# A hybrid decoder on one core: y groups copied out by ScalarE, exponentials held from the third query split, x's first tile issued first

## The chip, the core and the metric

The kernel runs on one core of one Trainium2 chip. The core has a matrix engine (TensorE, PE in the profile; its weight loads are PEld), a vector engine (VectorE, DVE), an activation engine (ScalarE, ACT), a general engine (GpSimd, POOL) and a queue engine that here only issues DMAs (SyncE, SP). Every engine works through its own instructions in a fixed order. The metric is the device time of one execution in microseconds; the figure of a kernel is the median of its runs.

## The reference

The input is x with 256 positions of 2048 features in float32. Two layers follow.

```
layer 0:  x += recurrent_block(rms_norm(x));  x += swiglu_ffn(rms_norm(x))
k, v   =  split(rms_norm(x) @ w_kv), k normalised per head        # 4 heads of 64
layer 1:  x += attention(rms_norm(x), k, v);  x += swiglu_ffn(rms_norm(x))
```

The recurrent block splits `rms_norm(x) @ w_in` in a y branch and an x branch of 2048 each. The x branch passes a causal convolution of width 4, two block diagonal gates with sigmoids, and a linear recurrence over the positions; its result times gelu(y) goes through `w_out`. Attention has 32 query heads of 64, each query normalised per head, a causal window of 128, and a sink per head in the softmax. The feed-forward width is 5632.

## The kernel before, in words

**Layout.** Features lie on the 128 partitions, the 256 positions along the free dimension, so a vector of 2048 features is 16 tiles of 128x256. A product in float32 is made of three products of a shorter format: each operand is split in a high part and the low remainder, and high times high, high times low and low times high are summed in a bank of PSUM. For an activation the split is `split_act` (L419): ScalarE copies the high part, VectorE subtracts. `gained` (L425) does the same with the norm's gain: it reads a tile of x and a column of the parameter tile `par`, ScalarE first, VectorE after it.

**The stream of weights.** All weights pass in 704 tiles of 128x1024 (512 KB), in one long list `jobs`. `stream` (L278) goes through it: `load` (L231) issues the DMA of the tile four ahead on SP's queue, `split` (L259) makes `hi` on ScalarE (L264) and `lo` on VectorE (L267) for the tile three ahead, and the job's own function issues 24 matmuls of 256 columns (L330, L328). Four buffers each hold `raw`, `hi` and `lo`. `warm` (L269) runs 15 matmuls on zeros before the first tile. In `load` for tile 0, ScalarE's queue issues two small DMAs: 16 columns of `par` (L238) and the first tile of x (L239).

**Groups.** `group` (L347) makes a group of 512 output features: 8 jobs (22 for the output of the feed-forward layer), at the end of which `done` gets four results in banks of PSUM; there are 8 banks. With a non-empty `sync`, the first two results of a group have two halves in one bank that must be added (`two`). `pull` (L401) takes a result out of its bank: with `two`, ScalarE copies one half and VectorE adds; without, VectorE multiplies by `rstd` straight from the bank if `r` is given, and ScalarE copies if not. Then the bank is free.

**The planner.** The work between matmuls is written as generators that are spawned in a list `bg`. `run_bg` (L203) steps the first one that is due, in the order of spawning, until the work issued in this tick, by estimated costs, passes `DVE_TICK` or `ACT_TICK`. A tick is half a job. A `yield` lets the budget be looked at, a `yield n` sets the generator aside for n ticks. If a job needs an operand that isn't issued yet, `need` (L216) steps all generators until it is. Program order is the priority from which the compiler's scheduler then fixes each engine's order, with its own estimate of when operands are ready.

**Recurrent block.** The order of jobs is `ORDER` (L54): x0 and x1 interleaved, x2, g0, x3, g1, y0, g2, g3, y1, g4, g5, y2, g6, g7, y3. x and y are groups, g are the gates, one job each (`gates`, L651), whose sigmoids free two banks per gate; `recur` (L684) then does the recurrence of two gates' tiles. `y_group` (L716) pulls its four results through `scaled` (L583), which multiplies by the norm's `rstd` once that is known, and its task computes gelu and the product with the recurrence (ScalarE's squares, VectorE's products, ScalarE's tanh, the final split). y0 and y2 have no `sync`, y1 and y3 have. The output projection (`lru_out`, `project`, L512) follows y3 at once and needs the split products in order.

**Attention.** `attn` (L868) has four groups of queries, each of four pairs of heads. At a group's end its task (L1012) squares the four results, splits them (`split_act`, L1022), sums the squares per head by small matmuls (L1031), copies the sums out with ScalarE into a tile `h` (L1034), transposes them on TensorE (L1039), makes the factors of the norm (`rsqrt`) and puts the four pairs in `todo`. The generator `pairs` (L946) visits TensorE every three ticks (`VISIT`): a visit issues the values of one pair (L881), the scores of a new one (L899) and the transposes of a third (L891). Between visits `softmax` (L910) takes the new pair: VectorE adds the mask and takes the row maximum (L918), ScalarE makes the exponentials (L929, L934), VectorE the reciprocal, GpSimd the sums and products (L940, L942). The flag `summing` stops the softmax before the maximum is negated (L925) while a query group's sums are on their way: it is set after the four splits (L1024) and cleared after the copy to `h` (L1035). The small float32 matmuls and transposes are issued through `pe_other` (L334), which keeps them in one chain. Most rows of the profile name a helper's line: L116 is every activation of ScalarE, L125, L129, L134 and L136 are VectorE's, L338 and L341 the small matmuls. The output projection of attention has its first two groups interleaved, so that a pair of value tiles is used for two jobs.

Of the kernel before, what the change touches and what calls it, by code (L numbers as in the profile page):

```python
# [15 lines left out]
ALU = mybir.AluOpType  # L16
# [3 lines left out]
T = 256  # L20
# [29 lines left out]
class Trunk:  # L50
# [180 lines left out]
    def load(self, i):  # L231
        dma = self.nc.sync.dma_start
        raw, src = self.raw[i % 4], self.jobs[i][0]
        if i == 0:

            other = self.nc.scalar.dma_start
            g = slice(C_N1A, C_N1A + 16)
            other(self.par[:, g], self.d["par"][:, g])  # L238
            other(self.x[0][:, 0:1, :], self.d["x"][:, 0:1, :])  # L239
            dma(raw[:, 0:512], src[:, 0:512])  # L240
            dma(self.x[0][:, 1:2, :], self.d["x"][:, 1:2, :])
            dma(raw[:, 512:1024], src[:, 512:1024])
        elif i == 1:
            dma(raw[:, 0:512], src[:, 0:512])
            dma(raw[:, 512:1024], src[:, 512:1024])
        else:
            dma(raw, src)

        if i == 0:
            self.xin = 2  # L250
        elif i % 2 and i < ND - 1:
            dma(self.x[(i + 1) // 4][:, (i + 1) % 4:(i + 1) % 4 + 2, :], self.d["x"][:, i + 1:i + 3, :])
            self.xin = i + 3
        elif i == 8:
            dma(self.par[:, C_N1A + 16:NPAR], self.d["par"][:, C_N1A + 16:NPAR])
        elif i == 10:
            dma(self.con, self.d["con"])
# [341 lines left out]
    def lru(self, gains, rn):  # L599
# [116 lines left out]
        def y_group(g):  # L716
            def done(ps):
                v = []
                for f in range(4):
                    o = self.half()  # L720
                    self.scaled(o, ps[f])
                    v.append(o)

                def task():
                    th = []
                    yield 1
                    for f in range(4):
                        s = self.slot(F32)
                        o = s[:, 0:T]
                        th.append((s, o))  # L730
                        self.a(o, v[f], AF.Square, scale=math.sqrt(0.044715 * GK))
                        yield
                    for f in range(4):
                        o = th[f][1]
                        self.stt(o, o, GK, v[f], ALU.add, ALU.mult)
                        self.a(o, o, AF.Tanh)
                        yield
                    for f in range(4):
                        s, o = th[f]
                        k = 4 * g + f  # L740
                        self.stt(o, o, 1.0, v[f], ALU.add, ALU.mult)
                        while not hs[k].ready:
                            yield 1
                        h = hs[k].ap[:, 0:T]
                        self.stt(o, o, 0.5, h, ALU.mult, ALU.mult)
                        yield
                        q = self.slot()
                        self.split_act(q, o)
                        self.free(s)
                        self.free(hs[k].ap)  # L750
                        self.free_half(v[f])
                        zs[k].ap = q
                        zs[k].ready = True
                        yield
                self.spawn(task())
            self.group(lambda c: w[g, c], ND, xs, done, g == 3, self.SYNC if g in (1, 3) else ())

# [110 lines left out]
    def attn(self, xs, r, gains, rn):  # L868
# [41 lines left out]
        def softmax(k, rr, ps, sc):  # L910
            f = k % 4
            sm = self.half()
            mx, nm, es, den = (sm[:, 4 * i:4 * i + 4] for i in range(4))
            for hh in range(2):
                for b, c0, c1 in blocks:
                    i = b * 2 + hh
                    self.dve += 69 + 1.042 * (c1 - c0)
                    nc.vector.tensor_tensor_reduce(  # L918
                        sc[hh][:, c0:c1], ps[hh][:, c0:c1], con[:, K_MASK + c0:K_MASK + c1],
                        rr[:, b * 8 + f * 2 + hh:b * 8 + f * 2 + hh + 1],  # L920
                        par[:, C_SINK + 4 * k + hh:C_SINK + 4 * k + hh + 1], ALU.add, ALU.max,
                        accum_out=mx[:, i:i + 1])
                self.free_mbank(ps[hh])
                yield
            while self.summing:  # L925
                yield 1
            self.ts(nm, mx, -1.0, None, ALU.mult)
            self.tt(es, par[:, C_SINK + 4 * k:C_SINK + 4 * k + 4], mx, ALU.subtract)
            self.a(es, es, AF.Exp)  # L929
            for hh in range(2):  # L930
                for b, c0, c1 in blocks:
                    i = b * 2 + hh
                    o = sc[hh][:, c0:c1]
                    self.a(o, o, AF.Exp, bias=nm[:, i:i + 1], accum_out=den[:, i:i + 1])  # L934
                yield
            self.tt(den, den, es, ALU.add)
            self.rcp(den, den)
            for hh in range(2):
                o = sc[hh][:, P:2 * P]
                nc.gpsimd.tensor_tensor(o, o, sc[hh][:, 2 * P:3 * P], ALU.add)  # L940
                o = sc[hh][:, 0:2 * P].rearrange("p (b q) -> p b q", b=2)
                nc.gpsimd.tensor_tensor(o, o, den[:, hh:4:2].unsqueeze(2).broadcast_to([P, 2, P]), ALU.mult)  # L942
                yield
            self.free_half(sm)
# [59 lines left out]
        for g in range(4):  # L1004
            def done(ps, g=g):
                v = []
                for p in ps:
                    s = self.slot(F32)
                    self.pull(p, s[:, 0:T])
                    v.append(s)  # L1010

                def task():  # L1012
                    while not self.rv[r].ready:
                        yield 1
                    rt = self.rstd[r][:, T:T + 2]
                    if g == 0:
                        self.stt(r2, rt, 1.0 / HD, rt, ALU.mult, ALU.mult)
                    qs = []
                    for f in range(4):
                        self.a(v[f][:, T:2 * T], v[f][:, 0:T], AF.Square)  # L1020
                        qs.append(self.slot())
                        self.split_act(qs[f], v[f][:, 0:T])  # L1022
                        yield
                    self.summing = True  # L1024
                    yield 1
                    while not self.room():
                        yield 1
                    p = self.mbank()

                    for f in range(4):  # L1030
                        self.pe_other(p[32 * f:32 * f + 32, 0:T], con[:, K_HS:K_HS + 32], v[f][:, T:2 * T],  # L1031
                                      start=True, stop=True)
                    h = self.half()
                    self.a(h, p[:, 0:T])  # L1034
                    self.summing = False  # L1035
                    yield
                    yield 1
                    for b in range(2):
                        self.pe_other(p[:, T + b * P:T + b * P + P], h[:, b * P:b * P + P], one, f=nc.tensor.transpose)  # L1039
                    self.free_half(h)  # L1040
                    yield 1
                    rr, m, t = (self.rrs[g][:, 16 * i:16 * i + 16] for i in range(3))
                    for b in range(2):
                        self.ts(m[:, 8 * b:8 * b + 8], p[:, T + b * P:T + b * P + P:16], r2[:, b:b + 1], EPS,
                                ALU.mult, ALU.add)
                    self.free_mbank(p)
                    for q in v:
                        self.free(q)
                    self.rsqrt(rr, m, t)
                    for b in range(2):  # L1050
                        self.ts(rr[:, 8 * b:8 * b + 8], rr[:, 8 * b:8 * b + 8], rt[:, b:b + 1],
                                1.0 / math.sqrt(HD), ALU.mult, ALU.mult)
                    yield
                    for f in range(4):
                        todo.append((4 * g + f, qs[f], rr))
                    if g == 0:
                        self.spawn(pairs())
                    yield
                self.spawn(task())
            self.group(lambda c, g=g: w[g, c], ND, xs, done, g == 3, self.SYNC, packed=True)  # L1060
# [100 lines left out]
```

## Time and profile before

| what | us |
|---|---|
| runs, median of three | 1982.1 (1980.66 to 1982.5) |
| the profiled execution, its own time | 1980.68 |
| its span, first to last instruction | 1978.9 |
| TensorE busy | 1971.8 |
| VectorE busy | 1256.3 |
| ScalarE busy | 1063.0 |
| GpSimd busy | 70.5 |

The granted clock of TensorE is 1.00 over the span. A row of a timeline gives start and length in us, engine, line and operation, the tiles written and read (`out<-in`, buffer numbers left out), shape and count, and in square brackets how long the engine sat idle just before and what ended that. Several instructions of one kind in a row are merged to one line. `b` is a bank of PSUM, `s` a general tile of 128x512, `h` a half-sized one. The recurrent block takes up to about 290 us, the first feed-forward layer lies behind it, attention with its projections between 1011 and 1270, and the second feed-forward layer takes the rest.

### The profile page before, as it was taken

The page shows a single profiled execution, that of the slowest core. Times are in us where ns is not written, and L with a number is a line of the kernel's source. Part 1 is how long each engine was busy: PE and PEld are TensorE (multiplying, and loading weights), DVE is VectorE, ACT ScalarE, POOL GpSimd, SP SyncE. Part 2 cuts the span into 40 slices and gives each one's busy share as a digit, 9 for nine tenths or more (in the row PEclk, how much of TensorE's full clock was granted, in tenths as well). Part 3 has the DMA queues.
Part 4 walks back from the last instruction along what each step waited for, and adds up shares of the span by engine and source line. Part 5 has one row for each costly group of instructions (what it writes and reads, how often), then busy time and mean ns, then how long its engine had stood idle before and what let it go on. Part 6 is the DMA issues. An engine that isn't in the chain of part 4 may idle for free.

```text
span 1978.9 us, 40162 instructions
## 1 busy us (share of the span) xinstructions
PE 1971.8 (100%) x16683; PEld 1930.5 (98%) x16683; DVE 1256.3 (63%) x1981; ACT 1063.0 (54%) x1606; POOL 70.5 (4%) x100
## 2 busy tenths in 40 slices
PE   9999999999999999999999999999999999999999
PEld 9999999999999999999999889999999999999999
DVE  8988876556556655545668776755655565554443
ACT  7798655444444444434556775544544454443342
POOL 0000000000000000000002461000000000000000
PEclk9999999999999999999999999999999999999999
DMA  8555655655556555555655335555565556666663
GB/s 289 185 180 189 212 190 190 197 194 192 192 194 195 196 192 193 192 195 196 195 183 180 130 128 168 190 196 192 192 193 196 196 190 196 193 195 204 208 205 126
DMA packets 106198, 377.10 MB, mean 191 GB/s; under 512 B 11936, under 2 KB 14368, under 8 KB 106016
## 3 DMA queue, kind: packets, MB, share of 16 engines
q1 hardware_dynamic: 105408, 373.88, 57.7%
q8 instruction: 130, 2.13, 0.4%
q10 hardware_dynamic: 608, 0.66, 0.1%
q14 instruction: 52, 0.43, 0.1%
HBM read 371.88 MB, written 2.10 MB: 189 GB/s over the span
## 4 chain that ended last, share of the span: by engine, by line
PE 97%; ACT 1%; DVE 1%; issue 0%; POOL 0%; DMA 0%; ACTq 0%; POOLq 0%
PE b L330 93%; PE b L341 1%; PE b L664 1%; ACT s L116 1%; PE b L338 1%; PE b L850 1%; DVE lo L267 0%; ACT hi L264 0%; DVE s L918 0%; PE b L859 0%; PE b L860 0%; PE b L861 0%; DMA x<-in_x 0%; DVE s L125 0%; DVE s L129 0%
## 5 line engine op out<-in xcount | busy, mean ns | idle before, releaser
L330 PE MATMUL b<-s,hi 128*128 128x256 f32 (+1 forms) x10329 | 1432.1, 284 | 1.1 <-DVE h L125 0.6
L330 PEld LDWEIGHTS b<-s,hi 128*128 128x128 f32 x10329 | 1316.8, 188 | 30.5 <-ACT s L116 1.2
L267 DVE TENSOR_TENSOR lo<-raw,hi 128x1024 fp32r<-128x1024 f32 (+1 forms) x707 | 861.5, 1220 | 655.0 <-ACT hi L264 652.6
L264 ACT ACTIVATE hi<-raw 128x1024 fp32r<-128x1024 f32 (+1 forms) x707 | 746.1, 1056 | 808.6 <-PE b L330 750.7
L330 PE MATMUL b<-s,lo 128*128 128x256 f32 x5504 | 827.9, 276 | 0.0
L330 PEld LDWEIGHTS b<-s,lo 128*128 128x128 f32 x5504 | 718.3, 188 | 0.6
L940 POOL TENSOR_TENSOR s<-s 128x128 f32<-128x128 f32 x32 | 14.8, 463 | 1100.4 <-ACT s L116 1097.6
L116 ACT ACTIVATE s<-h 128x256 fp32r<-128x256 f32 (+1 forms) x106 | 40.7, 411 | 23.5 <-DVE h L125 23.5
L116 ACT ACTIVATE t<-b 128x256 f32<-128x256 f32 x130 | 47.9, 375 | 4.1 <-PE b L330 1.7
L116 ACT ACTIVATE s<-x,par 128x256 fp32r<-128x256 f32 x80 | 38.9, 499 | 20.4 <-DVE x L125 13.7
L116 ACT ACTIVATE s<-s 128x256 f32<-128x256 f32 (+2 forms) x116 | 41.7, 412 | 10.9 <-DVE s L129 7.5
L116 ACT ACTIVATE h<-h 128x256 f32<-128x256 f32 (+1 forms) x104 | 38.9, 376 | 3.7 <-DVE h L125 1.5
L116 ACT ACT_TABLE_LOAD x30 | 38.5, 1283 | 0.6
L129 DVE SCALAR_TENSOR_TENSOR s<-x,par,s 128x256 fp32r<-128x256 f32 x80 | 37.6, 479 | 1.8 <-ACT s L116 1.2
L125 DVE TENSOR_TENSOR x<-x,b 128x256 f32<-128x256 f32 x64 | 24.1, 415 | 21.2 <-PE b L330 21.2
L125 DVE TENSOR_TENSOR h<-b,rstd 128x256 f32<-128x256 f32 x100 | 37.5, 414 | 0.0
L125 DVE TENSOR_TENSOR h<-h,rstd 128x256 f32<-128x256 f32 x94 | 35.3, 416 | 0.0
L125 DVE TENSOR_TENSOR s<-s,s 128x256 fp32r<-128x256 f32 (+2 forms) x84 | 32.4, 416 | 4.1 <-ACT s L116 4.0
L125 DVE TENSOR_TENSOR h<-h,h 128x256 f32<-128x256 f32 x88 | 34.7, 415 | 0.5 <-ACT h L116 0.5
L125 DVE TENSOR_TENSOR s<-h,s 128x256 fp32r<-128x256 f32 x88 | 34.9, 417 | 0.1
L125 DVE TENSOR_TENSOR h<-b,t 128x256 f32<-128x256 f32 x92 | 34.5, 415 | 0.0
L116 ACT ACTIVATE s<-s,h 128x128 f32<-128x128 f32 x64 | 28.2, 442 | 10.2 <-DVE h L134 5.2
(99 smaller groups left out, 612.0 us busy)
## 6 DMA issues: line engine op xcount, KB each, us to landing
raw<-in_ffn_in SPq DMA_DIRECT2D x352, 512.0 KB, 3.4
raw<-in_ffn_out SPq DMA_DIRECT2D x176, 512.0 KB, 3.5
raw<-in_lru_in SPq DMA_DIRECT2D x62, 512.0 KB, 3.8
raw<-in_lru_out SPq DMA_DIRECT2D x32, 512.0 KB, 4.1
raw<-in_w_q SPq DMA_DIRECT2D x32, 512.0 KB, 3.4
raw<-in_w_o SPq DMA_DIRECT2D x32, 512.0 KB, 3.3
raw<-in_gate SPq DMA_DIRECT2D x8, 512.0 KB, 3.7
raw<-in_kv SPq DMA_DIRECT2D x8, 512.0 KB, 4.3
```

The lines of the kernel that those rows point to most:

```text
L116: self.nc.scalar.activation(out, in_, func, **kw)
L125: self.nc.vector.tensor_tensor(out, a, b, op)
L129: self.nc.vector.scalar_tensor_tensor(out, a, s, b, op0, op1)
L264: high = self.ins(self.nc.scalar.activation(hi[:, q], raw[:, q], AF.Copy))
L267: self.nc.vector.tensor_tensor(lo[:, q], raw[:, q], hi[:, q].bitcast(F32), ALU.subtract)
L330: self.nc.tensor.matmul(*args, **kw)
L338: self.other = self.ins(f(*args, **kw))
L341: self.other = self.ins(f(*args, **kw))
L664: nc.tensor.matmul(out[j], (hi if high else lo)[:, c:c + P], x2[kt][:, q:q + T], start=kt == 0 and high > q, stop=kt == 1 and not high)
L850: nc.tensor.matmul(ps[f][:, 0:T], w0, x2[kt][:, q:q + T], start=k0 + kt == 0 and high > q, stop=k0 + kt == ND - 1 and not high)
L940: nc.gpsimd.tensor_tensor(o, o, sc[hh][:, 2 * P:3 * P], ALU.add)
```

## The change

Three places are edited. In `load`, the two DMAs on ScalarE's queue change places. In `y_group`, a group without `two` results (y0 and y2) is taken out of its banks by ScalarE copies, and its task multiplies by `rstd` in SBUF, one VectorE instruction and a `yield` for each result. In attention, `summing` is set inside the loop, as soon as the third of the four splits is issued, and each exponential of the softmax waits for the flag before it is issued.

```diff
             g = slice(C_N1A, C_N1A + 16)
+            other(self.x[0][:, 0:1, :], self.d["x"][:, 0:1, :])
             other(self.par[:, g], self.d["par"][:, g])
-            other(self.x[0][:, 0:1, :], self.d["x"][:, 0:1, :])
...
         def y_group(g):
             def done(ps):
                 v = []
+                plain = not ps[0][1]
                 for f in range(4):
                     o = self.half()
-                    self.scaled(o, ps[f])
+                    if plain:
+                        self.pull(ps[f], o)
+                    else:
+                        self.scaled(o, ps[f])
                     v.append(o)
 
                 def task():
                     th = []
                     yield 1
+                    if plain:
+                        for o in v:
+                            self.tt(o, o, self.rstd[0][:, 0:T], ALU.mult)
+                            yield
                     for f in range(4):
...
                     o = sc[hh][:, c0:c1]
+                    while self.summing:
+                        yield 1
                     self.a(o, o, AF.Exp, bias=nm[:, i:i + 1], accum_out=den[:, i:i + 1])
...
                         self.split_act(qs[f], v[f][:, 0:T])
+                        self.summing = f > 1
                         yield
-                    self.summing = True
                     yield 1
```

## The prediction

> **What bounds the kernel now.** I read the page first, then TensorE's waits, then busy time by stretches, and last the timeline round each wait.
>
> ```profile
> span 1978.9 us, 40162 instructions
> ...
> PE 1971.8 (100%) x16683; PEld 1930.5 (98%) x16683; DVE 1256.3 (63%) x1981; ACT 1063.0 (54%) x1606; POOL 70.5 (4%) x100
> ```
>
> TensorE is busy for 1971.8 of 1978.9 us. The change adds and removes no matmul, so this number cannot move; only the time in which TensorE stands still can. The second view lists that time, releaser by releaser (total, times, longest, in us):
>
> ```profile
> PE b L338 <- ACT h L116: 1.2, 1, 1.2
> PE b L275 <- DVE lo L272: 1.2, 1, 1.2
> PE b L330 <- DVE h L125: 0.6, 2, 0.4
> PE b L330 <- ACT s L116: 0.5, 1, 0.5
> PE b L338 <- POOL s L984: 0.3, 1, 0.3
> ```
>
> This is the whole purse: 3.8 us, 0.19% of the span. The 1.2 of L275 is the wait for the first memset and 0.3 is a wait for GpSimd; no edit touches either. That leaves one wait for each edit: 0.5 us at the first matmul (the tile order at the start), 0.6 us on `h<-b,rstd` (the y groups), 1.2 us on the copy `h` (the exponentials). I treat them in the order of time, because a gain early on only lasts if the engines that feed TensorE later can keep up. Whether they can, the busy times by stretch say (columns: stretch, its length, then PE, PEld, DVE, ACT, POOL busy with their counts, clock, DMA share, GB/s):
>
> ```profile
> 170.00:183.00 13.00, 12.36 (x106) 11.99 (x106) 12.97 (x28) 11.15 (x24) 0.00 (x0) 1.00 0.69 220
> 183.00:203.00 20.00, 20.00 (x165) 19.60 (x164) 18.45 (x38) 19.94 (x38) 0.00 (x0) 1.00 0.51 170
> 203.00:225.50 22.50, 22.50 (x192) 22.13 (x191) 22.50 (x42) 16.79 (x30) 0.00 (x0) 1.00 0.57 191
> ```
>
> Between 170 and 225 us VectorE idles for 0.03, 1.55 and 0.00 us. Here it is as full as TensorE, though over the whole span it is busy for 63% only.
>
> **Edit 1, x's first tile ahead of the parameter tile.** Both are issued from ScalarE's queue; the first `gained` needs both.
>
> ```profile
> 0.75 0.41 ACTq L238 DMA_DIRECT2D par<-in_par  x1
> ...
> 1.19 0.44 ACTq L239 DMA_DIRECT2D x<-in_x  x1
> ...
> 3.81 0.63 ACT L264 ACTIVATE hi<-raw 128x512 fp32r<-128x512 f32 x1 [0.86 <-DMA raw<-in_lru_in]
> ...
> 4.68 0.91 ACT L116 ACTIVATE s<-x,par 128x256 fp32r<-128x256 f32 x2 [0.24 <-DMA x<-in_x]
> ...
> 5.24 1.49 PE L330 MATMUL b<-s,hi 128*128 128x256 f32 x6 [0.49 <-ACT s L116]
> ```
> ```profile
> x<-in_x ACTq DMA_DIRECT2D x1, 128.0 KB, 3.4
> par<-in_par ACTq DMA_DIRECT2D x1, 8.0 KB, 3.2
> ```
>
> x lands at 1.19+3.4 = 4.59, and ScalarE, free since 3.81+0.63 = 4.44, waits 0.24 us for it. Swapped, x is issued at 0.75 and lands near 4.15; the parameters are issued near 1.19 and land at 4.39 with their own 3.2, at 4.59 with the 3.4 of the other row. Neither is later than x is now, and ScalarE is not free before 4.44. So the gain lies between 0.24 (by 3.2) and 0.00 (by 3.4). I take 0.2, since 3.2 is this tile's own row. No instruction is added, and SP's queue issues the same as before.
>
> [...]
>
> **Edit 2, the y groups.** Only y0 and y2 are `plain` (y1 and y3 have synchronised tiles with two halves per bank). For each, four VectorE multiplies that read the bank become four ScalarE copies and four later VectorE multiplies in SBUF.
>
> ```profile
> L125 DVE TENSOR_TENSOR h<-b,rstd 128x256 f32<-128x256 f32 x100 | 37.5, 414 | 0.0
> L125 DVE TENSOR_TENSOR h<-h,rstd 128x256 f32<-128x256 f32 x94 | 35.3, 416 | 0.0
> ...
> L116 ACT ACTIVATE h<-b 128x256 f32<-128x256 f32 x6 | 2.2, 374 | 0.3 <-PE b L341 0.3
> ```
>
> VectorE's work stays: 8 x 414 out, 8 x 416 in. ScalarE gets 8 x 374 ns = 3.0 us more, half at each group. What the move buys is earlier free banks. At y0 (ends near 121 us) no TensorE wait is on the list, so nothing is to be had. At y2 there is:
>
> ```profile
> 175.38 0.42 ACT L116 ACTIVATE s<-s 128x256 f32<-128x256 f32 x1 [0.77 <-DVE s L129]
> ...
> 179.93 0.74 DVE L125 TENSOR_TENSOR h<-b,rstd 128x256 f32<-128x256 f32 x2
> ...
> 180.44 0.72 ACT L116 ACTIVATE s<-h 128x256 f32<-128x256 f32 x2 [1.03 <-DVE h L125]
> ...
> 180.92 0.28 PE L664 MATMUL b<-s,lo 128*128 128x256 f32 x1
> 180.93 0.41 DVE L125 TENSOR_TENSOR h<-b,rstd 128x256 f32<-128x256 f32 x1
> ...
> 181.49 0.47 PE L330 MATMUL b<-s,hi 128*128 128x256 f32 x2 [0.29 <-DVE h L125]
> 181.86 0.39 DVE L125 TENSOR_TENSOR h<-b,rstd 128x256 f32<-128x256 f32 x1
> ...
> 182.31 0.98 PE L330 MATMUL b<-s,hi 128*128 128x256 f32 x6 [0.35 <-DVE h L125]
> ```
>
> VectorE comes to the four pulls at 179.93 to 182.25, and y3's first matmuls write the banks that the last two of them free. From 180.92 to 182.31 TensorE starts three matmuls, one of L664 and two of L330, in 1.39 us; at 4.24 us for 36 (a row further down) three take 0.35. So 1.04 us is lost. ScalarE has two holes just before (0.77 and 1.03 us); copies put there free the banks well ahead of 181, and the 1.04 goes.
>
> What is late next? The split of the streamed weights. Tile by tile, ScalarE makes `hi` and VectorE `lo`; here is the start of the stretch in which VectorE never rests, and the tightest tile in it, the fourth of lru_out:
>
> ```profile
> 190.69 1.04 ACT L264 ACTIVATE hi<-raw 128x1024 fp32r<-128x1024 f32 x1
> ```
> ```profile
> 191.76 1.23 DVE L267 TENSOR_TENSOR lo<-raw,hi 128x1024 fp32r<-128x1024 f32 x1 [1.55 <-ACT hi L264]
> ...
> 212.10 1.21 DVE L267 TENSOR_TENSOR lo<-raw,hi 128x1024 fp32r<-128x1024 f32 x1
> ```
> ```profile
> 213.56 1.07 PE L330 MATMUL b<-s,lo 128*128 128x256 f32 x8
> ```
>
> That `lo` is ready at 212.10+1.21 = 213.31 and used at 213.56: margin 0.25. If TensorE arrives 1.04 earlier and VectorE does not, TensorE waits 0.79 there, and y2's net gain is 0.25. VectorE's chain back from 213.31 has no hole until 191.76, where it waited for the `hi` of 190.69. So net gain = 0.25 + d, with d how much earlier that `hi` comes, up to 1.04 in all. ScalarE before it had holes of 0.77+1.03 = 1.80 and gets 4 x 0.374 = 1.50. If the copies lie in the holes, d = +0.30; if none does, d = -1.50. I take d = +0.15, half of the upper end, because the holes stand where the copies become ready and a fixed order will not fill them exactly. **Net 0.4 us**, ends -1.25 and 0.55.
>
> [...]
>
> **Edit 3, the exponentials.** `summing` now rises with the third split instead of after the fourth, and each exponential asks for it.
>
> ```profile
> 1160.17 0.17 DVE L134 TENSOR_SCALAR h<-h 128x4 f32<-128x4 f32 x1
> ...
> 1160.38 0.40 ACT L116 ACTIVATE s<-s,h 128x128 f32<-128x128 f32 x1 [1.73 <-DVE h L134]
> ...
> 1160.87 0.36 ACT L116 ACTIVATE h<-b 128x256 f32<-128x256 f32 x1
> ...
> 1161.29 0.33 PE L338 MATMUL b<-con,h 128*128 128x128 f32 x1 [1.21 <-ACT h L116]
> ```
>
> In ScalarE's order an exponential stands ahead of the copy of the query sums, waits 1.73 us for its row maximum, and the copy, and TensorE's transposes behind it, wait with it. With the exponentials held until the copy is issued, the copy goes in that 1.73 us hole, and TensorE's 1.21 goes. The exponentials lose at most the copy's 0.36 us, since the maximum isn't there before 1160.34. Queued behind the new wait is the pair's own chain: its denominators on VectorE, its multiplies on GpSimd, and the next visit of `pairs`, which starts only when that chain has been issued. The cost is bounded below by nothing and above by the rival on visits. At the other three groups' sums TensorE waits for no copy, so nothing is gained there. I take **1.2 us**.
>
> **Sum.** 0.2 + 0.4 + 1.2 = 1.8 us. The profiled execution took 1980.68 us, 1.8 around its span of 1978.9: 1978.9 after. The median of the three runs, 1982.1, stands 1.4 above that execution, and the forecast for a median is 1982.1 - 1.8 = **1980.3 us**, -0.09%. A measurement of this kernel can tell about 0.2% (4 us) from no change, so I forecast no change that can be told.
>
> **Rivals.** (a) *Everything is kept*: VectorE keeps up at 213 us, and 0.2 + 1.04 + 1.2 = 2.4 goes: 1979.7. For it: 1.55 us of VectorE hole at 191.76 that could close. Against it: the margin of 0.25.
> (b) *The hold does not do what it says*: the planner's order still puts something slow ahead of the copy, or the exponential was issued before the third split; 1.2 stays, 0.6 goes: 1981.5.
> (c) *The copies push the splits*: d = -1.50; -0.2 + 1.25 - 1.2 = -0.15: 1982.0. For it: ScalarE is busy 19.94 of 20 us from 183. Against it: the two holes.
> (d) *The held exponentials make the visits late* (slower). Each visit comes 36 matmuls after the one before; the values of the last pair are needed by w_o's first groups:
>
> ```profile
> 1186.36 4.24 PE b L330 x36
> ```
> ```profile
> 1203.13 0.42 DVE L125 TENSOR_TENSOR s<-b,s 128x256 fp32r<-128x256 f32 x1 [1.22 <-ACT s L116]
> ```
> ```profile
> 1206.94 0.40 PE L330 MATMUL b<-s,hi 128*128 128x256 f32 x2
> ```
>
> The last value is there at 1203.55, the tile that uses it begins at 1206.94: 3.39 us in hand. From a slip of more than that, so from one visit (4.24), `need` forces visits out with no matmuls between them, and up to the 4.24 us that now cover a visit stands bare, twice if two are forced: 8.5 - 1.8 = +6.7, 1988.8. Against it: the pair held at 1160 is transposed two visits later, and the next visit waits for the query sums anyway.
>
> **Chances.** Forecast 0.62, (a) 0.15, (b) 0.13, (c) 0.05, (d) 0.05. Runs of one kernel spread from 1980.66 to 1982.5, about 0.9 to either side, so the range goes from (a) less 1.0 to (c) plus 0.8: 1978.7 to 1982.8; it leaves out (d) and the tails. Faster by over 0.2% would need more than the whole list of waits: 0.04, for the spread alone. Slower by over 0.2%: (d) and a little of the spread, 0.06. Within: 0.90.
>
> **What would show it.** Edit 1: the first L330 matmul starts near 5.04 instead of 5.24; if it is later, the parameters were late behind x. Edit 2: four `h<-b` copies on ScalarE near 175 to 179 and no TensorE wait near 181; then a TensorE wait of some tenths for `lo` near 212 is my give-back, and none means (a). Edit 3: the copy `h` ahead of the exponential near 1160 and no 1.2 in the waits; the last matmul of the attention visits no later than 1202. The prediction is wrong if a wait over 1 us stands anywhere in TensorE's list except the memset's, or if the first two groups of w_o wait for values.

## The result: slower by 0.2%

After the change the median is **1985.1 us** (20 runs, 1984.04 to 1987.54); the kernel before, run beside it, has 1980.88 (20 runs, 1980.12 to 1983.23). The ratio is 1.0020, 95% interval 1.0014 to 1.0026. The forecast was 1980.3 with a range up to 1982.8: the time lies outside it, on the slow side, at the border of the slowdown by over 0.2% that got a chance of 0.06. The profiled execution took 1984.25 us with a span of 1982.4, 3.6 us more than the 1980.68 and 1978.9 of before.

The runs fall in two groups, in before about 1.8 us apart (1980.12 to 1981.08, and 1982.10 to 1983.23), so where a single microsecond matters I compare the lower groups. That of after is 1984.04 to 1984.72: the change costs about 3.6 us. The 1982.1 from which the forecast subtracted its 1.8 was a median of three, two of them from the upper group; from the 1980.88 of all 20 runs the same terms would have given 1979.1.

The page of after first, its span and its busy times:

```profile
span 1982.4 us, 40166 instructions
...
PE 1973.0 (100%) x16683; PEld 1931.1 (97%) x16683; DVE 1256.3 (63%) x1981; ACT 1065.9 (54%) x1614; POOL 70.5 (4%) x100
```

The work is what the diff says: ScalarE has 8 instructions more (1606 to 1614) and 2.9 us more of busy time, VectorE the same number and the same time. Nothing here explains 3.6 us. TensorE's waits explain most of it, 6.0 us against 3.8, and TensorE's busy time, which grew by 1.2 us with the same number of matmuls, the rest (releaser, total, times, longest):

```profile
PE b L330 <- ACT hi L264: 2.2, 2, 1.6
PE b L338 <- ACT h L116: 1.2, 1, 1.2
PE b L275 <- DVE lo L272: 1.2, 1, 1.2
PE b L330 <- DVE s L125: 0.6, 1, 0.6
PE b L338 <- POOL s L994: 0.3, 1, 0.3
PE b L330 <- ACT s L116: 0.3, 1, 0.3
PE b L330 <- ACT h L116: 0.2, 1, 0.2
```

Compare it with the list in the prediction. The 1.2 on the copy `h`, which edit 3 was to remove, stands there unchanged. The 0.6 on `h<-b,rstd` is gone, but two waits for `hi` (2.2) are new, and so is one for a product `s` on VectorE (0.6).

To place the loss, I summed for each stretch the time from each matmul's start to the next start, less 0.4427 ns per column, the pace at which all 4.41 million columns take 1952.7 us (113 ns for a matmul of 256 columns). What is left is time that TensorE lost: waits, small matmuls, and stretches of a slower pace (us; the last column is the whole run from the first matmul to the last, and the differences in it are those of the spans):

```
stretch (us)      0-12  170-186  186-204  204-250  1145-1175  1175-1230   all
before            2.98     1.27     0.41     0.05       3.40       3.30  21.47
after             3.81     0.61     1.69     2.37       3.21       3.59  25.05
banks_turned      2.95     0.01     1.06     0.77       3.40       3.29  21.34
y2_alone          3.43     0.49     1.69     2.19       3.27       3.51  24.18
y2_at_once        2.92     1.03     0.54     0.89       3.25       3.31  21.77
copy_first        2.95     1.28     0.39     0.05       1.83       3.82  20.21
hold_alone        2.91     1.19     0.01     0.61       3.25       3.29  21.10
```

From before to after, the head loses 0.83 us, the stretch from 170 to 250 us loses 2.94 (4.67 against 1.73), and attention loses 0.10. So edit 2 cost most, edit 3 did nothing, and edit 1 cost something. The other rows belong to the experiments. The last one says how finely the table can be read: hold_alone turns out to be the program of before, executed again, and it differs by up to 0.56 us in a stretch and by 0.37 in all. The heads of y2_alone, 3.43, and of y0_alone, 3.30, whose start is that of before, put edit 1's part at 0.4 to 0.9 us.

The slower pace is not in the prediction. Behind the waits here, matmuls of 256 columns start 118 ns apart instead of 113 for some time: in before from the wait at 181 us to 197 us, in after to 198 us, then from 203 to 221 and from 227 to 236 us, each time behind a wait. Of the 2.94 us that after loses more between 170 and 250 us, 2.05 are waits and 0.89 are this pace. What makes it no run tests.

**The head of after**, in its timeline. Square brackets are the idle time just before and its end:

```profile
0.74 0.41 ACTq L238 DMA_DIRECT2D x<-in_x  x1
...
1.19 0.44 ACTq L239 DMA_DIRECT2D par<-in_par  x1
...
4.42 0.42 ACT L116 ACTIVATE acc<-x 128x256 f32<-128x256 f32 x1 [1.48 <-DMA x<-in_x]
...
4.91 0.91 ACT L116 ACTIVATE s<-x,par 128x256 fp32r<-128x256 f32 x2
...
5.72 2.18 ACT L264 ACTIVATE hi<-raw 128x512 fp32r<-128x512 f32 x4
...
6.38 1.21 PE L330 MATMUL b<-s,hi 128*128 128x512 f32 x6 [1.63 <-ACT hi L264]
```

The DMAs are swapped as meant. But x, now issued first, is there only at 4.42, and ScalarE's order is another one. Before, the first `hi` came first, at 3.81 us, before x was there. Now ScalarE sits idle for x, squares it for the norm (`acc<-x`), makes two `gained`, and only then, at 5.72, the first `hi`. The first matmul starts at 6.38 instead of 5.24.

**The stretch of y2 in after**, ScalarE's timeline and then VectorE's:

```profile
180.15 0.91 ACT L116 ACTIVATE h<-b 128x256 f32<-128x256 f32 x3
180.94 1.06 ACT L264 ACTIVATE hi<-raw 128x1024 fp32r<-128x1024 f32 x1
181.89 0.38 ACT L116 ACTIVATE h<-b 128x256 f32<-128x256 f32 x1
183.38 0.42 ACT L116 ACTIVATE s<-h 128x256 f32<-128x256 f32 x1 [1.11 <-DVE h L125]
184.29 0.42 ACT L116 ACTIVATE s<-h 128x256 f32<-128x256 f32 x1 [0.50 <-DVE h L125]
184.73 1.28 ACT L116 ACT_TABLE_LOAD   x1
186.03 1.57 ACT L116 ACTIVATE s<-b,par 128x256 f32<-128x256 f32 x4
187.47 1.07 ACT L264 ACTIVATE hi<-raw 128x1024 fp32r<-128x1024 f32 x1
```
```profile
182.93 0.42 DVE L125 TENSOR_TENSOR h<-h,rstd 128x256 f32<-128x256 f32 x1
183.26 0.68 DVE L709 TENSOR_TENSOR_SCAN s<-s,s 128x256 f32<-128x256 f32 x1
183.86 0.40 DVE L125 TENSOR_TENSOR h<-h,rstd 128x256 f32<-128x256 f32 x1
```

The copies left three banks by 181.06 us, where before had the third at 181.34, and the fourth at 182.27 as in before (182.25); TensorE's wait for them went from 0.6 to 0.2 us. But the squares (`s<-h`) don't read the copies, they read the scaled tiles, and VectorE makes those behind its scans, at 182.93 and 183.86; before, the multiplies from the bank began at 179.93. ScalarE, in its fixed order, stands still 1.61 us for them, and behind the squares stand the table load, four sigmoids and the `hi` of weight tile 66. That `hi` comes at 187.47. In before the same two rows, on ScalarE, read:

```profile
182.74 1.28 ACT L116 ACT_TABLE_LOAD   x1
...
185.48 1.07 ACT L264 ACTIVATE hi<-raw 128x1024 fp32r<-128x1024 f32 x1
```

So the whole chain is 1.99 us later. TensorE pays twice, the second time far behind:

```profile
188.59 1.08 PE L330 MATMUL b<-s,hi 128*128 128x256 f32 x4 [0.61 <-ACT hi L264]
...
226.17 0.39 PE L330 MATMUL b<-s,hi 128*128 128x256 f32 x1 [0.26 <-ACT s L116]
227.19 0.39 PE L330 MATMUL b<-s,hi 128*128 128x256 f32 x1 [0.64 <-DVE s L125]
```

The pair at 226 and 227 us waits for the last products of y3, on lru_out. VectorE, which makes them, has no hole from 193.75 us on in after (from 191.76 in before), and in its order the last scans of the recurrence now stand behind y3's four pulls (from 210.80) instead of ahead of them (from 210.10). No run separates the later start from the order. First the row of before, then the two of after:

```profile
207.80 1.27 DVE L709 TENSOR_TENSOR_SCAN s<-s,s 128x256 f32<-128x256 f32 x2
```
```profile
213.93 1.26 DVE L709 TENSOR_TENSOR_SCAN s<-s,s 128x256 f32<-128x256 f32 x2
...
216.90 0.68 DVE L709 TENSOR_TENSOR_SCAN s<-s,s 128x256 f32<-128x256 f32 x1
```

**Attention in after** is as it was, an exponential ahead of the copy and the transposes behind the copy:

```profile
1163.95 0.40 ACT L116 ACTIVATE s<-s,h 128x128 f32<-128x128 f32 x1 [1.72 <-DVE h L134]
...
1164.45 0.36 ACT L116 ACTIVATE h<-b 128x256 f32<-128x256 f32 x1
...
1164.87 0.33 PE L338 MATMUL b<-con,h 128*128 128x128 f32 x1 [1.20 <-ACT h L116]
```

### The profile page after: what moved, and what is told of

The parts are those of the page before. It is cut to its first block, busy times and chain, and to the rows that moved or that the text cites. A ratio compares the mean times of both kernels' runs of the same rounds, so it can differ in the third digit from the quotient of the medians.

```text
span 1982.4 us, 40166 instructions
## 1 busy us (share of the span) xinstructions
PE 1973.0 (100%) x16683; PEld 1931.1 (97%) x16683; DVE 1256.3 (63%) x1981; ACT 1065.9 (54%) x1614; POOL 70.5 (4%) x100
## 4 chain that ended last, share of the span: by engine, by line
PE 95%; DVE 2%; ACT 2%; issue 1%; DMA 0%; POOL 0%; ACTq 0%; DVEq 0%; POOLq 0%
PE b L330 91%; PE b L341 1%; ACT s L116 1%; PE b L664 1%; DVE lo L267 1%; PE b L338 1%; PE b L858 1%; ACT hi L264 0%; DVE s L129 0%; DVE s L125 0%; ACT L116 0%; DVE s L926 0%; DVE s L709 0%; PE b L868 0%; PE b L867 0%
```

## The experiments

Three questions: is the loss of the head the queue or the order; is the loss of y2 the copies' work or the place of the multiplies; and why did the hold not move the copy? Every kernel is the kernel before with the edit that is shown, in its main lines. The times are those of the lower group, the ratios are to runs of before on the same chip.

### head_alone: edit 1 by itself

```diff
+            other(self.x[0][:, 0:1, :], self.d["x"][:, 0:1, :])
             other(self.par[:, g], self.d["par"][:, g])
-            other(self.x[0][:, 0:1, :], self.d["x"][:, 0:1, :])
```

> Only the swap of the two first DMAs of ScalarE's queue. Theory: about 0.8 us slower than before, TensorE's first product near 6.4 instead of 5.24 us with a wait of 1.6 us for hi, because the scheduler now places the first split of weights behind the work on x. Rival 1 (my prediction): 0.2 us faster, first product near 5.04. Rival 2: the parameters land late behind x, the first scaled tile of x begins at 5.0 or later although ScalarE is free, and the loss is 0.4.

Measured: 1981.07 to 1981.44 (three runs of 11; the other eight are 1982.59 to 1983.36); ratio 1.0004, interval 0.9996 to 1.0013. By the three that is about 0.5 us slower, which the interval doesn't separate from nothing. ScalarE's order is that of after, with `acc<-x` first:

```profile
4.38 0.42 ACT L116 ACTIVATE acc<-x 128x256 f32<-128x256 f32 x1 [1.43 <-DMA x<-in_x]
...
5.68 1.13 ACT L264 ACTIVATE hi<-raw 128x512 fp32r<-128x512 f32 x2
```

So the swap alone changes the order of instructions that the diff doesn't touch. That leaves open how much of the loss is that order and how much the parameters' later landing.

### head_hi_first: the swap, with the first split held ahead of the work on x

The kernel also issues the second half of the first split behind the two `gained`, and holds the norm's square behind the split of the second tile.

```diff
+            if i == 0 and c == 0:
+                self.firsthi = high
...
-            if k in (2, 3) and self.opening is not None:
-                with self.tc.issue_after(self.opening):
+            if k in (0, 1) or self.opening is not None and k in (2, 3):
+                with self.tc.issue_after(self.opening if k > 1 else self.firsthi):
...
+                with self.tc.issue_after(self.opening):
+                    self.a(self.acc, xt, AF.Square)
```

> Before with x's first tile issued ahead of the parameters, and order edges that keep ScalarE's and VectorE's order of before at the start (first half of the weights' split, then the two tiles of x, then the second half). Theory: the loss of the swap alone comes from the scheduler's new order and not from the DMAs, so TensorE's first product stands at 5.0 to 5.3 us again and the time is that of before or up to 0.2 us less. Rival: the parameters land later behind x; then the first tile of x is scaled at 4.9 instead of 4.68 and TensorE starts near 5.5, 0.2 us later than before.

Measured: the lowest three 1980.56 to 1980.90, ratio 1.0002, interval 0.9993 to 1.0012. The 0.5 us is gone, but nothing is won over before (one further run took 4035 us and is left out):

```profile
4.10 0.63 ACT L264 ACTIVATE hi<-raw 128x512 fp32r<-128x512 f32 x1 [1.15 <-DMA raw<-in_lru_in]
...
4.80 0.91 ACT L116 ACTIVATE s<-x,par 128x256 fp32r<-128x256 f32 x2
...
5.36 2.19 PE L332 MATMUL b<-s,hi 128*128 128x256 f32 x6 [0.60 <-ACT s L116]
```

TensorE's first product is at 5.36 instead of head_alone's 6.35, and the first 12 us lose 4.50 us instead of 5.30: the order made most of the loss. Which of the three held instructions matters is not separated. The `gained` still start at 4.80, not before the 4.68 of before. In this profile the weight tile came late too (the split waits for `raw` until 4.10), so it doesn't say what the swap would bring if nothing else moved.

### y0_alone and y2_alone: edit 2 for one group each

```diff
-                plain = not ps[0][1]
+                plain = g == 0
```

The second has `g == 2`; the rest of edit 2 is as in the change.

> Only y0 is copied out by ScalarE and scaled later, y2 as before. Theory: no change within 0.5 us, no new wait of TensorE between 99 and 170. Rival: the loss of the y groups is here, about 2.5 us.

> Only y2 is copied out by ScalarE and scaled later, y0 as before. Theory: all of the 2.5 us that both y groups cost comes from y2, in the stretch from 170 to 230 us where VectorE never rests, so about 2.5 us slower than before. Rival: y0's copies push a full ScalarE between 121 and 148 us, and the loss is theirs; then y2 alone costs nothing.

Measured: y0_alone 1980.61 to 1981.17, ratio 1.0001 (0.9992 to 1.0011); y2_alone 1983.26 to 1983.88, ratio 1.0014 (1.0005 to 1.0024). Both groups together, the kernel **y_alone**, gave this against its own expectation:

> Only the y groups: y0 and y2 copied out by ScalarE and scaled later. Theory: about 2.7 us slower than before, with TensorE waits near 187, 202 and 225 us that before does not have, since the loss of the whole change beside the head's 0.8 lies there. Rival (my prediction): 0.4 us faster, no wait near 181, at most some tenths near 212.

1982.69 to 1983.73, ratio 1.0011 (1.0002 to 1.0020). So edit 2's loss of 2 to 3 us is y2's. y0_alone has no new wait, as expected; in its profile the slower pace runs from 154 to 197 us, which y_alone, with the same edit of y0, doesn't show. The waits of y2_alone hold the same new entries as those of after:

```profile
PE b L330 <- DVE s L125: 0.6, 1, 0.6
PE b L330 <- ACT hi L264: 0.6, 1, 0.6
```

### y2_at_once and y2_no_scale: late multiplies, or the copies' own work?

My theory from after's timeline: the multiplies are late, because each stands behind a step of the planner, and so behind scans. The rival: four more activations ahead of the `hi` of tile 66 are enough. The first kernel issues each multiply right behind its copy; the second leaves the multiplies out. The lines are the difference of the first from y2_alone.

```diff
                     if plain:
                         self.pull(ps[f], o)
+                        self.tt(o, o, self.rstd[0][:, 0:T], ALU.mult)
...
-                    if plain:
-                        for o in v:
-                            self.tt(o, o, self.rstd[0][:, 0:T], ALU.mult)
-                            yield
```

> The kernel before with the group y2 alone copied out by ScalarE, and each of its four multiplies by 1/rms issued right behind its copy, with no step of the planner between. Theory L (late multiplies: with a planner's step ahead of each, the multiplies stand behind scans on VectorE, the squares wait for them, and the table load, the sigmoids and the split of tile 66 stand behind the squares): the multiplies come forward, the split of tile 66 is back within 0.4 us of where it was, TensorE waits less than 0.4 us for it, and the time is 1980.5 to 1981.5, against 1983.3 to 1983.8 for y2 alone. Theory W (the work itself: four more activations of 0.36 us ahead of the split of tile 66 on ScalarE, in whatever order): the split stays about 1.2 us later, the wait of 0.8 us for it stays, and the time is 1982.7 to 1983.8.

> The kernel before with the group y2 alone copied out by ScalarE, and its four multiplies by 1/rms left out: this kernel does not compute that scaling. VectorE then has four instructions fewer than in y2 alone (4 x 0.41 us), and the squares need the copies alone. Theory L (late multiplies): no wait of the squares for VectorE, split of tile 66 within 0.4 us of where it was, time 1980 to 1981.3. Theory W (the copies' own time on ScalarE): the split of tile 66 stays 1 us or more later, TensorE still waits 0.5 us or more for it, time 1982 to 1983.5.

Measured: y2_at_once 1980.93 to 1981.57, ratio 1.0004 (0.9995 to 1.0013); y2_no_scale 1980.87 to 1981.58, ratio 1.0003 (0.9994 to 1.0012). ScalarE makes the same four copies in both, so the copies' work costs 0.5 us at most, by intervals that include nothing, and the place of the multiplies, with the planner's step ahead of each, cost the other 2 and more. The timeline of y2_at_once on VectorE and ScalarE, and TensorE over the place where after waited 0.61 us:

```profile
179.82 0.75 DVE L125 TENSOR_TENSOR h<-h,rstd 128x256 f32<-128x256 f32 x2
```
```profile
180.27 0.42 ACT L116 ACTIVATE s<-h 128x256 f32<-128x256 f32 x1 [0.77 <-DVE h L125]
...
182.81 1.28 ACT L116 ACT_TABLE_LOAD   x1
...
185.54 1.08 ACT L264 ACTIVATE hi<-raw 128x1024 fp32r<-128x1024 f32 x1
```
```profile
186.16 2.75 PE L330 MATMUL b<-s,hi 128*128 128x256 f32 x19
```

The first multiplies start at 179.82, as in before (179.93) and not as in after (182.93). The table load stands at 182.81, where before had it at 182.74; the `hi` of tile 66 at 185.54 against 185.48; and the nineteen matmuls from 186.16 run without a wait. TensorE itself is 0.45 us earlier here than in before (its tile 63 starts at 177.87 against 178.32), so the `hi` is 0.5 us late by that measure, and the stretch from 170 to 250 us loses 2.46 us here, 0.7 more than in before.

### banks_turned: is the wait at 181 us worth anything?

The copies were to free the banks for y3 sooner. This kernel gets the same without any copy: y3's first two results take the two banks that are freed first.

```diff
                         ps = [self.bank() for _ in range(4)]
+                        if turn:
+                            ps = ps[2:] + ps[:2]
```

> Before, with y3 taking y2's four banks in another order, so that its first products use the banks that VectorE frees first; every engine's order of instructions stays that of before. The wait of about 1 us near 181 should go. My prediction's rule of the give-back says that the lo of the weights is then late in lru_out, and TensorE waits some 0.8 us near 212 to 223, so that only 0.25 us are saved. Rival: VectorE keeps up and 1.0 us is saved.

Measured: 1980.23 to 1981.08, ratio 1.0001 (0.9992 to 1.0011). TensorE runs through at 181 us, and pays in small waits from 186 us on, the longest at 213:

```profile
180.81 1.07 PE L330 MATMUL b<-s,hi 128*128 128x256 f32 x8
...
213.14 1.09 PE L330 MATMUL b<-s,lo 128*128 128x256 f32 x7 [0.21 <-DVE lo L267]
```

In the table of lost time, 1.26 us goes from 170 to 186 and 1.37 comes back from 186 to 250 (against hold_alone 1.18 and 1.21). So removing the stall at 181 us won nothing: ScalarE and VectorE, not TensorE, set the pace from 170 to 225 us (in before VectorE idles for 1.58 us there, and ScalarE is busy for 19.94 of the 20 us from 183 to 203), and the stall was only the place where TensorE waited for them.

### hold_alone: edit 3 by itself

```diff
+                    while self.summing:
+                        yield 1
                     self.a(o, o, AF.Exp, bias=nm[:, i:i + 1], accum_out=den[:, i:i + 1])
...
+                        self.summing = f > 1
                         yield
-                    self.summing = True
```

> Only the hold on the exponentials is taken from the change. Theory: the hold does nothing, because the last query group's copy h already stood ahead of that pair's exponentials in the order in which the kernel issues them, and it is the compiler's scheduler that moves one exponential ahead of it; then the engines' orders are those of before, the 1.2 us wait of TensorE for h stays, and the time is that of before within 0.5 us. Rival (my prediction): the copy goes first, the 1.2 us wait is gone, and the time is 1.2 us less.

Measured: 1980.20 to 1981.13, ratio 0.9999 (0.9990 to 1.0008; one further run took 7079 us and is left out), and TensorE's longest wait stays:

```profile
PE b L338 <- ACT h L116: 1.2, 1, 1.2
```

Row by row, the order of the instructions on every engine is that of before; the built program is the same, instruction for instruction. The hold is not violated, it is empty: in the order in which the kernel issues the last query group, the copy `h` already stands ahead of the pair's exponentials, since the old flag stops that pair's softmax until the copy is issued. What puts an exponential ahead of the copy is the step behind it, the compiler's scheduler. That it does so by its estimate of when operands are ready is not shown here.

### copy_first: the order that edit 3 meant, as an order

```diff
+                    self.copied = self.ins(nc.scalar.activation(h, p[:, 0:T], AF.Copy))
...
+            edge, self.copied = self.copied, None
+            behind = lambda: self.tc.issue_after(edge) if edge is not None else ExitStack()
...
+                    with behind():
+                        self.a(o, o, AF.Exp, bias=nm[:, i:i + 1], accum_out=den[:, i:i + 1])
```

> Before, with one thing added: the exponentials of the pair that follows a query group's copy h are tied behind that copy by an order edge, so the scheduler cannot put one ahead. Theory (ScalarE's fixed order makes the wait): the wait of TensorE for h, 1.2 us near 1160, is gone and 1.0 to 1.2 us are saved. Rival: the copy would wait or be late for another reason, or the held exponentials make the later visits late; then nothing is saved or the time grows.

The pair's small exponential on the sinks is held in the same way. Measured: 1979.38 to 1980.85, ratio 0.9995 (0.9986 to 1.0005). The copy, and the head of TensorE's waits (lines of helpers are one higher in this kernel):

```profile
1158.15 0.39 ACT L1040 ACTIVATE h<-b 128x256 f32<-128x256 f32 x1
```
```profile
PE b L276 <- DVE lo L273: 1.2, 1, 1.2
PE b L339 <- POOL s L989: 0.8, 2, 0.5
```

The copy comes at 1158.15, ahead of the exponentials at 1160; in before it stood behind one, at 1160.87. The 1.2 is gone, and the wait for GpSimd grows from 0.3 to 0.8. In the table, 1.57 us goes between 1145 and 1175 and 0.52 comes back behind it, a net 1.05. That is the forecast's term for edit 3 nearly to size, from an order that edit 3 doesn't make. Against before the lower group is about 0.8 us faster; the interval doesn't separate that from nothing.

### first_and_turned and all_mended: put together

The first is copy_first with banks_turned. The second is all three edits in their mended forms: the head with its first split held, y0 and y2 with multiplies at once, and copy_first. Their diffs are those above.

> The two edits that were harmless or gained, together: the copy of the first sums ahead of the exponentials by an order between instructions, and y3's banks turned so that its first products go to the free ones. If the stages are independent, the gains add: copy first took 1.3 us from the profiled span (1977.6 against 1978.9) and the turned banks 0.2 (1978.7), so a span of about 1977.4 and a time of 1979.2 to 1979.8 among the lower times. Rival: what the turned banks take at 181 us is given back at 186 and 213 us in full, and the time is that of the copy first alone, 1979.4 to 1980.2.

> The three edits of the change together, each in the form that showed no loss or the least: x's tile issued ahead of the parameter tile with the first split held ahead of the work on x; y0 and y2 copied out by ScalarE with each multiply issued right behind its copy; the copy of the first sums held ahead of the exponentials by an order between instructions. If what was found of each part alone holds in the whole, the lower times are those of before (1980.2 to 1981.1) with about 0 for the head, +0.4 for y2 and -0.9 for the copy: 1979.4 to 1980.7, so about 4 us under the change as it was made (1984.0 to 1984.7). Rival: the parts work on each other (a shift at the head moves each later wait by its own amount), and the time is 1981 to 1983.

Measured: first_and_turned 1979.58 to 1980.58, ratio 0.9998 (0.9989 to 1.0007); all_mended 1980.91 to 1981.36, ratio 1.0002 (0.9993 to 1.0011). The rival held for the first: it is no better than copy_first, so the turned banks are given back in full. The second lies some 3 us under after, but above its own expected 1979.4 to 1980.7 and at the edge of its rival's 1981 to 1983. The copy's gain is there (attention loses 1.02 us less than in before), and from 170 to 250 us the waits are down from 1.16 us to 0.16. What uses this up is the slower pace, which runs from 154 to 197 us and for most of 202 to 234, and takes 2.0 us more than in before between 60 and 250 us. Whether the edits bring it on is not shown. No version here is shown to beat before by more than can be measured; copy_first has the lowest times.

## Why the prediction was wrong

**What bounds the kernel.** Right: TensorE, and a purse of a few us of waits. TensorE's busy time, which "cannot move", moved all the same, by 1.2 us with the same matmuls. What the purse hid is that it bounds a gain and not a loss. I had a full VectorE and a ScalarE busy 19.94 of 20 us in the very stretch that edit 2 loads, and still took small numbers on both sides.

**Edit 1, -0.2 forecast, about +0.4 to 0.9 measured.** Two steps failed. "Neither is later than x is now": in after both transfers take longer to land.

```profile
x<-in_x ACTq DMA_DIRECT2D x1, 128.0 KB, 3.7
...
par<-in_par ACTq DMA_DIRECT2D x1, 8.0 KB, 3.7
```

x, issued at 0.74, is there at 4.42 and not near 4.15. The parameters, issued at 1.19, land near 4.89 by their 3.7, 0.3 us later than x did before. No run shows a price of 0.4 us for 8 KB behind 128 KB, which was head_alone's second rival: there the first `gained` starts at 4.87, not at 5.0 or later. In after the parameters' row moved by 0.5 (3.2 to 3.7), but x's own moved by 0.3 (3.4 to 3.7) with nothing ahead of it, and y2_alone has 3.7 for the parameters in the old order too. In the four kernels with the swap the parameters take 0.0 to 0.1 us more than x, in the others 0.1 to 0.5 less. The larger failure is what the step did not ask: "ScalarE is not free before 4.44" took ScalarE's order as given. With the swap, the scheduler put x's square and both `gained` ahead of the first split; my guess, which no run tests, is that it takes x to be there earlier. head_hi_first shows that order to be most of the loss.

**Edit 2, -0.4 forecast, +2.9 measured in after's own stretch.** The step "if the copies lie in the holes, d = +0.30" failed. The holes of 0.77 and 1.03 us were not free time for copies: each was ScalarE waiting for VectorE in a fixed order, and the change made the second wait longer (1.61 us in two pieces), because the multiplies for which the squares wait came 3 us later, behind scans. The step had counted the multiplies' work ("VectorE's work stays") and put their place in VectorE's order at nothing. The rule itself, net gain = 0.25 + d, is not confirmed. With banks_turned d is about 0, and 0.25 was due; the profile shows 0.2 by its span (1978.7 against 1978.9) and -0.1 by the table of that stretch, both within what a second execution of one program moves (0.4 between before and hold_alone). In after, the `hi` of 190.69 comes at 192.68; TensorE enters the stretch 0.67 us later than before (0.83 from the head, 0.16 made up by 170 us), so d is -1.3 and the rule gives a loss of 1.1 where 2.9 was measured. A negative d is the rival *the copies push the splits*, to which I gave 0.05, and even it ended at 1982.0. It was priced by ScalarE's work (4 x 0.374) when the price was in the order: y2_at_once and y2_no_scale do the copies' work for 0.5 at most. And the rule followed only the weight splits. The products at 226 us (1.33 us of lost time: 0.42 and 0.91) come from a second chain through VectorE, with the recurrence's scans in it, that I did not follow; the slower pace (0.89 us) is the other part that it lacks. From the bank and from SBUF the multiply takes about as long in after too, 414 and 417 ns.

**Edit 3, -1.2 forecast, 0 measured.** The failed step: "With the exponentials held until the copy is issued, the copy goes in that 1.73 us hole." Held in the program's order they were already. The rival *the hold does not do what it says* had this ("the planner's order still puts something slow ahead of the copy"), at 0.13; it is the scheduler's order, not the planner's. The size, 1.2, was nearly right (1.05 in copy_first). The visits are not late: the last value is there at 1207.13 in after and its tile is used at 1210.52, 3.39 us in hand as before.

**The signs I named.** A wait over 1 us stands in the list beyond the memset's: 1.6 on the first `hi`, and the old 1.2. The first matmul came later than 5.24, and I had put that to the parameters alone.

## What to carry to other kernels

A program's order is only advice where a scheduler stands behind it: before you price a moved instruction, ask what else the move lets the scheduler reorder (here the swap of two DMAs moved the first `hi` from 3.81 to 5.68 us in head_alone), and if an order matters, write it as an order between two instructions and look for it in the timeline. A hole on a fixed-order engine has an owner: if the engine waits for another one there, work put in front of it fits only when the awaited result doesn't move, and here it moved by 3 us because the multiplies, each behind a step of the planner, came behind scans. Where two feeding engines are full, a stall of the engine that they feed is a symptom; take it away by itself (as the turned banks do, with 1.26 us gone and 1.37 back) and see whether it comes back later, before paying for it.

## What the hardware showed that I had not expected

About 2 us of a run are decided in its first ten. In y_alone, whose profiled execution took 1985.01 where its fastest runs took 1982.69, TensorE does far fewer matmuls in its first microseconds than before does (columns: stretch, its length, PE, PEld, DVE, ACT, POOL busy with counts, clock, DMA share, GB/s). First y_alone, then before:

```profile
7.00:9.00 2.00, 2.00 (x12) 2.00 (x11) 1.33 (x4) 1.19 (x3) 0.00 (x0) 1.00 0.99 364
```
```profile
7.00:9.00 2.00, 2.00 (x19) 2.00 (x18) 1.17 (x2) 0.74 (x2) 0.00 (x0) 1.00 0.93 338
```

Twelve matmuls against nineteen between 7 and 9 us, with TensorE busy throughout and the granted clock at 1.00 in both. In y_alone a matmul of 256 columns starts every 213 ns from 8.11 to 9.81 us, in before every 118 ns from 6.3 us on. Of the 14 profiles five (y_alone, head_alone, head_hi_first, y2_no_scale, first_and_turned) have 10 to 12 matmuls there, and of these y_alone comes to 118 ns by 10.47 us and head_alone by 10.39; the other nine have 19 or 20. The five are those whose profiled execution lies in the upper group, and the first 12 us lose 4.92 us in y_alone against 2.98 in before. What makes the start slow in some executions and not in others, and what ends it, no run tests.
